# Placing the larger half of the ranked experts nine places apart instead of one

## The chip, the cores and the metric

The kernel runs on one core of one Trainium2 chip. The metric is the device time of one execution in microseconds (us); lower is shorter. A measurement is the median of several executions.

## What is computed

The reference is one layer of a diffusion backbone: a token mixer (retention and mLSTM over 512 latent tokens) followed by a mixture of experts. Only the second half matters here:

```
p_g = softmax(u @ w_rg + b_rg); g_idx = top_k(p_g, 1)
le  = (u @ w_re + b_re) of that group's 8 experts
pe_top, e_idx = top_k(softmax(le), 2)          # 2 experts of 32 for each of 512 tokens
expert(x) = (silu(x @ w_e1[e]) * (x @ w_e3[e])) @ w_e2[e]
out = sum over a token's two experts of weight * expert(token)
```

So 1,024 assignments are spread over 32 experts, unevenly, and the order in which experts are worked off is free. Each expert has three weight matrices of 2 MB in float32.

## The kernel before

The token mixer fills the first 1,000 us or so. Then comes a routing part (who goes to which expert), then a loop over 32 *places* `e`, each of which works one expert off, then the combination of the results and the last norm.

**A place.** An expert's tokens are cut into blocks of 32. The number of blocks, `n`, is read at run time into a register; every place has code for one block, and branches over the code for a second, a third and further blocks. A block is: `hidden_q` (line 1483: one pass of 64 matrix instructions over `w_e1` and `w_e3`), an activation, a small transpose (line 1473), and `output_q` (line 1494: 32 matrix instructions over `w_e2`). The first two blocks' tokens are fetched three places ahead by an indirect gather (`fetch_both`, tile `xr`); tokens of a third and further block are fetched inside the place (`rows`, tile `xo`). Results are stored to `y_d` by GpSimd's queue (lines 1651 and 1654, and 1514 for a third and further block). At the end of a conditional part each engine waits and branches; lines 1519, 1523, 1643 and 1652 are such ends and line 1629 is the load of the next place's `n`.

**The weights.** `load(n)` (line 949) issues load `n` of 96 on SyncE's queue (SP), in the order of the places, three loads a place, into a ring of 11 buffers. Load `3e + 11` and the two after it are issued when place `e` has released its buffers, so loads run up to about three and a half places ahead; and a load waits for the landing of the load three before it, so at most three are under way. For places from 4 on the expert's number is read from the tile `place[0]`.

**The order of the places.** Places 0 to 3 are experts 0 to 3 (`SET` is 4). The other 28 experts are ranked by their number of tokens, largest first, in ranks 4 to 31 (tile `ov`). The larger half, ranks 4 to 17, takes the even places 4, 6, ..., 30 in rank order; the smaller half, ranks 18 to 31, takes the odd places from 31 down to 5. So a large and a small expert alternate and the largest come first. The ranks become places in a dozen VectorE instructions on tiles of 128x32 (lines 1566 to 1572); from the places follow `yrow` and `pos` (where an assignment's result and its token number are kept), a scatter of the token numbers (line 1595, GpSimd), their reading back (line 1617), the gathers, and `place`.

Of the kernel before, what the change touches and what calls it, by code (L numbers as in the profile page):

```python
# [12 lines left out]
I32 = mybir.dt.int32  # L13
AF = mybir.ActivationFunctionType
OP = mybir.AluOpType
# [4 lines left out]
P = 128  # L20
# [5 lines left out]
NE = 32  # L26
# [3 lines left out]
SET = 4  # L30
# [38 lines left out]
def build(tc, I, out, dbg=None):  # L69
    nc = tc.nc  # L70
    V, S, G, PE, SP = nc.vector, nc.scalar, nc.gpsimd, nc.tensor, nc.sync
# [856 lines left out]
    loads, place, turn_of = [], [], {}  # L928
# [67 lines left out]
    eoff = moec.tile([P, NE], F32, name="eoff")  # L996
# [423 lines left out]
    m1p = mo.enter_context(tc.tile_pool(name="m1p", bufs=1, reuse_waits="tile"))  # L1420
# [10 lines left out]
    def slots_in(n, b):  # L1431

        xT = slots_of(b)
        for a in range(4):
            V.tensor_copy(xT[:, :, a, :], xg[a][:, :, n, 32 * b:32 * b + 32])
        return xT
# [99 lines left out]
    with tc.manual_schedule(engines={EN.DVE}):  # L1536
        xnext = [slots_in(0, b) for b in range(2)]
        ov = m1p.tile([P, NE], F32, tag="ov", name="ov")
        V.tensor_scalar(ov, nblk, -2.0, 0.0, op0=OP.add, op1=OP.max)
        V.scalar_tensor_tensor(ov, ov, 0.5, ov, op0=OP.is_gt, op1=OP.add)  # L1540
        nil = m1p.tile([P, NE], F32, tag="nil", name="nil")
        V.memset(nil, 0.0)
        V.tensor_tensor_scan(obase, ov, nil, 0.0, op0=OP.add, op1=OP.add)
        V.tensor_sub(obase, obase, ov)
        V.tensor_scalar(ocol, obase, 2.0 * NE, None, op0=OP.add)
        V.tensor_scalar(obase, obase, 32.0, 64.0 * NE, op0=OP.mult, op1=OP.add)

        key = m1p.tile([P, NE], F32, name="key")
        V.scalar_tensor_tensor(key, cnt, 2048.0, eoff, op0=OP.mult, op1=OP.subtract)
        V.tensor_scalar(key[:, 0:SET], eoff[:, 0:SET], -1.0, 1.0e7, op0=OP.mult, op1=OP.add)  # L1550
        val = m1p.tile([P, NE], F32, name="val")
        V.tensor_scalar(val, ocol, 1024.0, None, op0=OP.mult)
        V.scalar_tensor_tensor(val, nblk, 32.0, val, op0=OP.mult, op1=OP.add)
        V.scalar_tensor_tensor(val, eoff, 1.0 / 64, val, op0=OP.mult, op1=OP.add)

        def beside(a, b, n):

            return (a.rearrange("p (i o) -> p i o", o=1).to_broadcast([P, n, NE]),
                    b.rearrange("p (o j) -> p o j", o=1).to_broadcast([P, n, NE]))

        for a in range(2):
            h = slice(16 * a, 16 * a + 16)
            M = mr.tile([P, 16, NE], F32, tag="yt", name="M", bufs=YB)
            V.tensor_tensor(M, *beside(key[:, h], key, 16), op=OP.is_lt)
            V.reduce_sum(ov[:, h], M, axis=AX.X)
        V.tensor_scalar(nil, ov, SET - 0.5, None, op0=OP.is_gt)
        V.scalar_tensor_tensor(nil, ov, float(-SET), nil, op0=OP.add, op1=OP.mult)
        V.tensor_scalar(key, ov, (NE + SET) / 2 - 0.5, None, op0=OP.is_gt)
        V.tensor_scalar(eoff, ov, -4.0, 2.0 * (NE + SET) - 1, op0=OP.mult, op1=OP.add)
        V.tensor_mul(key, key, eoff)  # L1570
        V.tensor_add(ov, ov, nil)
        V.tensor_add(ov, ov, key)
        V.tensor_scalar(eoff, ov, 64.0, None, op0=OP.mult)
        sel = m1p.tile([P, 3, 8], F32, name="sel")
        rr = mr.tile([P, 8, NE], F32, tag="yq", name="rr", bufs=1)
        E8 = Ea.rearrange("p i k e -> p (i k) e")
        for a, src in enumerate((eoff, obase)):
            V.tensor_mul(rr, E8, src.rearrange("p (o e) -> p o e", o=1).to_broadcast([P, 8, NE]))
            V.reduce_sum(sel[:, a, :], rr, axis=AX.X)
        r8 = rank.rearrange("p i k -> p (i k)")  # L1580
        V.scalar_tensor_tensor(sel[:, 1, :], sel[:, 1, :], -64.0, sel[:, 0, :], op0=OP.add, op1=OP.subtract)
        V.tensor_scalar(sel[:, 2, :], r8, 63.5, None, op0=OP.is_gt)
        V.tensor_mul(sel[:, 1, :], sel[:, 1, :], sel[:, 2, :])
        V.tensor_add(sel[:, 0, :], sel[:, 0, :], sel[:, 1, :])
        V.tensor_add(yrow.rearrange("p i k -> p (i k)"), sel[:, 0, :], r8)
        rb8 = m1p.tile([P, 8], I32, name="rb8")
        V.tensor_copy(rb8, r8)
        V.tensor_scalar(rb8, rb8, 5, None, op0=OP.logical_shift_right)
        V.tensor_scalar(sel[:, 0, :], sel[:, 0, :], 1.0 / 32, None, op0=OP.mult)
        V.scalar_tensor_tensor(sel[:, 0, :], r8, float(NC), sel[:, 0, :], op0=OP.mult, op1=OP.add)  # L1590
        pos = m1p.tile([P, 8], I32, name="pos")
        V.scalar_tensor_tensor(pos, rb8, 1.0 - 32 * NC, sel[:, 0, :], op0=OP.mult, op1=OP.add)
# [7 lines left out]
    with tc.manual_schedule(engines={EN.DVE}):  # L1600
        V.tensor_scalar(ov, ov, 1.0, None, op0=OP.add)
        for a in range(2):
            h = slice(16 * a, 16 * a + 16)
            M = mr.tile([P, 16, NE], F32, tag="yt", name="M", bufs=YB)
            at, by = beside(iota[:, h], ov, 16)
            V.tensor_tensor(M, at, by, op=OP.is_equal)
            V.tensor_mul(M, M, beside(iota[:, h], val, 16)[1])
            V.reduce_sum(key[:, h], M, axis=AX.X)
        place += [m1p.tile([P, NE], I32, name=f"place{a}") for a in range(3)]
        V.tensor_copy(place[0], key)  # L1610
        V.tensor_scalar(place[1], place[0], 5, None, op0=OP.logical_shift_right)
        V.tensor_scalar(place[2], place[0], 10, None, op0=OP.logical_shift_right)
        V.tensor_scalar(place[0], place[0], 31, None, op0=OP.bitwise_and)
        V.tensor_scalar(place[1], place[1], 31, None, op0=OP.bitwise_and)
# [140 lines left out]
```

## Time and profile before

| | |
|---|---|
| three executions | 1661.69, 1650.82, 1650.40 us |
| median | 1650.82 us |
| the profiled execution | 1648.84 us |
| its span, first to last instruction | 1647.2 us |
| TensorE busy (matmul) | 1336.8 us, 81% of the span |
| VectorE / ScalarE / GpSimd busy | 773.8 / 425.8 / 296.3 us |
| moved by DMA | 355.31 MB, of it 96 weight loads of 2,048 KB |

The profile comes from one execution. Its page gives busy times, the span in 40 equal slices (41.2 us each), the DMA queues, and groups of instructions by line. Other views of the trace list single instructions in order of time, who waited for whom, and the busy time in chosen stretches. Times in those views count from the first instruction. PE is TensorE, DVE VectorE, ACT ScalarE, POOL GpSimd; a name with a q behind it (PEq) is that engine's instruction sequencer, and an idle time put down to it was ended by a branch, a semaphore or a register instruction, not by a tile.

### The profile page before, as it was taken

How to read it: one execution, taken by the hardware profiler on the slowest of the kernel's cores; microseconds unless marked ns; L12 is line 12 of the kernel's file. 1: busy time of each engine (PE TensorE's matmuls, PEld its weight loads, DVE VectorE, ACT ScalarE, POOL GpSimd, SP SyncE). 2: the span in 40 equal slices, each digit the busy share in tenths (PEclk: the TensorE clock that was granted, in tenths of full speed). 3: DMA queues.
4: the chain of work that ended last, by engine and by line, in shares of the span. 5: the costliest groups of instructions: out<-in, count | busy, mean ns of one | idle time of the engine just before them, and what ended most of it. 6: DMA issues, size and time to landing. Idle time of an engine off the chain costs nothing. (4 is left out here: it accounts for less than half of the span.)

```text
span 1647.2 us, 27521 instructions
## 1 busy us (share of the span) xinstructions
PE 1336.8 (81%) x10733; PEld 1029.2 (62%) x10733; DVE 773.8 (47%) x1857; ACT 425.8 (26%) x764; POOL 296.3 (18%) x249
## 2 busy tenths in 40 slices
PE   5999899999999999999998965556757666666574
PEld 3797888989798998989886753223323333333331
DVE  6657366485656566564778796111111111111115
ACT  3432244253444444444433120000000000000001
POOL 0100055143100000000012243222221211212103
PEclk9999999999999999999999977778888789988887
DMA  9414985243412122121655685955669999999974
GB/s 350 132 60 121 298 251 167 75 158 119 111 60 71 58 90 65 58 71 52 211 173 184 230 348 209 394 207 196 238 269 402 372 404 374 403 375 410 408 297 156
DMA packets 160928, 355.31 MB, mean 216 GB/s; under 512 B 24476, under 2 KB 111724, under 8 KB 152472
## 3 DMA queue, kind: packets, MB, share of 16 engines
q1 hardware_dynamic: 147736, 328.40, 54.6%
q0 software_dynamic: 11632, 19.54, 3.5%
q10 hardware_dynamic: 1296, 4.19, 0.6%
q8 instruction: 125, 2.05, 0.5%
q14 instruction: 139, 1.14, 0.2%
HBM read 316.34 MB, written 35.69 MB: 214 GB/s over the span
## 5 line engine op out<-in xcount | busy, mean ns | idle before, releaser
L1483 PE MATMUL ps_h<-w,xT 128*32 128x256 f32 x3072 | 222.8, 446 | 102.9 <-PEq L1629 49.9
L1483 PEld LDWEIGHTS ps_h<-w,xT 128*32 128x32 f32 x3072 | 123.0, 128 | 205.8 <-issue 127.3
L194 DVE TENSOR_TENSOR w_lo<-raw,w_hi 128x1024 fp32r<-128x1024 f32 x96 | 129.1, 1368 | 30.3 <-ACT w_hi L193 30.3
L1464 ACT ACTIVATE t<-ps_h 64x256 f32<-64x256 f32 x48 | 18.1, 377 | 480.3 <-PE ps_h L1483 429.2
L1452 DVE COPY xT<-ps_x 128x256 f32<-128x256 f32 x63 | 26.3, 417 | 231.9 <-PE ps_x L1450 222.5
L1494 PE MATMUL ps_y<-w,hT 128*32 128x256 f32 x1536 | 117.9, 459 | 20.4 <-ACT hT L1475 17.5
L193 ACT ACTIVATE w_hi<-raw 128x1024 fp32r<-128x1024 f32 x96 | 96.1, 1050 | 62.1 <-PE ps_t L214 18.0
L907 POOL TENSOR_TENSOR raw<-raw,g 128x2048 f32<-128x2048 f32 x4 | 18.6, 4642 | 451.9 <-DMA brw<-br_d 417.7
L557 POOL TENSOR_TENSOR macc<-macc,mw 128x1024 f32<-128x1024 f32 x32 | 79.6, 2487 | 96.8 <-ACT mw L556 88.7
L1496 DVE TENSOR_TENSOR yt<-ps_y,g2q 128x256 f32<-128x256 f32 x43 | 18.2, 424 | 165.9 <-PE ps_y L1494 131.5
L1494 PEld LDWEIGHTS ps_y<-w,hT 128*32 128x32 f32 x1536 | 52.0, 126 | 63.2 <-ACT hT L1475 23.3
L1442 POOL DMA_INDIRECT xr<-u_d,inv x56 | 58.0, 1036 | 181.8 <-DMA y_d<-yt 57.1
L213 PE MATMUL ps_q<-u_lat,w_hi 128*128 128x512 f32 x192 | 79.5, 414 | 2.4 <-ACT u_lat L319 1.7
L214 PE MATMUL ps_q<-u_lat,w_hi 128*128 128x512 f32 x192 | 78.8, 410 | 0.0
L215 PE MATMUL ps_q<-u_lat,w_lo 128*128 128x512 f32 x192 | 78.4, 409 | 0.0
L1473 PE MATMUL ps_ht<-small,t 64*128 64x64 f32 x96 | 15.2, 239 | 76.9 <-DVE t L1466 72.7
L213 PE MATMUL ps_v<-w_hi,u_lat 128*128 128x256 f32 x256 | 72.1, 282 | 0.0
L214 PE MATMUL ps_v<-w_lo,u_lat 128*128 128x256 f32 x256 | 72.1, 282 | 0.0
L215 PE MATMUL ps_g<-w_hi,u_lat 128*128 128x256 f32 x256 | 72.1, 282 | 0.0
L215 PE MATMUL ps_v<-w_hi,u_lat 128*128 128x256 f32 x256 | 72.1, 281 | 0.0
L213 PE MATMUL ps_g<-w_hi,u_lat 128*128 128x256 f32 x256 | 72.1, 281 | 0.0
L214 PE MATMUL ps_g<-w_lo,u_lat 128*128 128x256 f32 x256 | 72.0, 281 | 0.0
(429 smaller groups left out, 3433.9 us busy)
## 6 DMA issues: line engine op xcount, KB each, us to landing
w<-in_w_e_dram SPq DMA_DIRECT2D x96, 2048.0 KB
raw<-in_w_in_dram SPq DMA_DIRECT2D x40, 1024.0 KB
mw<-in_w_ada_dram SPq DMA_DIRECT2D x32, 512.0 KB
y_d<-plain SPq DMA_DIRECT2D x28, 512.0 KB
wada<-in_w_ada_dram SPq DMA_DIRECT2D x4, 2048.0 KB
y_d<-yt POOLq DMA_DIRECT2D x43, 128.0 KB
tanh_d<-tg SPq DMA_DIRECT2D x16, 256.0 KB
br_d<-rt SPq DMA_DIRECT2D x16, 256.0 KB
```

The costliest lines, as they stand in the source:

```text
L193: S.activation(h_, r_, AF.Copy)
L194: V.tensor_sub(l_, r_, f32(h_))
L213: PE.matmul(ps, lh, rh, start=first, stop=False)
L214: PE.matmul(ps, lh, rl, start=False, stop=False)
L215: PE.matmul(ps, ll, rh, start=False, stop=last)
L557: G.tensor_add(acc, acc, w)
L907: G.tensor_mul(raw, raw, g1.rearrange("p (o f) -> p o f", o=1).to_broadcast([P, NK, 256]))
L1442: G.indirect_dma_start(out=xr, out_offset=None, in_=u_d, in_offset=bass.IndirectOffsetOnAxis(ap=at, axis=0), bounds_check=4 * T - 1, oob_i ...
L1452: V.tensor_copy(xT.rearrange("p c a s -> p c (a s)"), pt)
L1483: PE.matmul(ps[32 * a:32 * a + 32, 0:256], x[:, kt % 2, kt // 2, :], w[a // 2][:, kt, 256 * (a % 2):256 * (a % 2) + 256], start=(kt == 0), ...
L1494: PE.matmul(py[32 * a:32 * a + 32, 0:256], hT[:, kt % 2, 32 * (kt // 2):32 * (kt // 2) + 32], w2[:, kt, 256 * a:256 * a + 256], start=(kt ...
L1496: V.tensor_mul(yq, py[:, 0:256], g2q)
```

## The change

The odd places and places 0 to 3 stay as they are. Among the larger half, rank `4 + j` goes to place `4 + 2 * (9 j mod 14)` in place of `4 + 2 j`. The even places 4, 6, ..., 30 thus hold ranks 4, 15, 12, 9, 6, 17, 14, 11, 8, 5, 16, 13, 10, 7, where before they held ranks 4, 5, 6, ..., 17. The quotient of `9 j` by 14 is computed with a multiplication and a shift in an integer tile; for that the three `place` tiles are made earlier, and the first of them is used as scratch.

```
@@ after the ranks are counted into ov
+        place += [m1p.tile([P, NE], I32, name=f"place{a}") for a in range(3)]
+        ninths = place[0]
+        V.tensor_scalar(ninths, ov, 9.0 * 4682, -9.0 * 4682 * SET, op0=OP.mult, op1=OP.add)
+        V.tensor_scalar(ninths, ninths, 16, None, op0=OP.logical_shift_right)
         V.tensor_scalar(nil, ov, SET - 0.5, None, op0=OP.is_gt)
-        V.scalar_tensor_tensor(nil, ov, float(-SET), nil, op0=OP.add, op1=OP.mult)
+        V.tensor_scalar(eoff, ov, 17.0, SET - 18.0 * SET, op0=OP.mult, op1=OP.add)
+        V.scalar_tensor_tensor(eoff, ninths, -28.0, eoff, op0=OP.mult, op1=OP.add)
+        V.tensor_mul(nil, nil, eoff)
         V.tensor_scalar(key, ov, (NE + SET) / 2 - 0.5, None, op0=OP.is_gt)
-        V.tensor_scalar(eoff, ov, -4.0, 2.0 * (NE + SET) - 1, op0=OP.mult, op1=OP.add)
+        V.scalar_tensor_tensor(eoff, ov, 3.0, eoff, op0=OP.mult, op1=OP.add)
+        V.tensor_scalar(eoff, eoff, -1.0, 2.0 * NE + 3, op0=OP.mult, op1=OP.add)
         V.tensor_mul(key, key, eoff)
         V.tensor_add(ov, ov, nil)
         V.tensor_add(ov, ov, key)
@@ further down, where place is filled
-        place += [m1p.tile([P, NE], I32, name=f"place{a}") for a in range(3)]
         V.tensor_copy(place[0], key)
```

## Rows read from the trace of the kernel before

**Rows 1.** The page's 40 slices: busy share of the DMA engines, in tenths

```profile
DMA  9414985243412122121655685955669999999974
```

**Rows 2.** Busy times by stretch: stretch, length, engines, granted clock, DMA share, GB/s

```profile
1091.70:1129.50 37.80, 22.68 (x338) 11.63 (x334) 6.23 (x15) 2.62 (x8) 11.88 (x20) 0.91 0.12 33
...
1170.00:1184.60 14.60, 11.12 (x102) 4.83 (x102) 1.79 (x5) 0.65 (x2) 2.42 (x4) 0.63 0.06 20
1184.60:1221.30 36.70, 18.67 (x302) 11.09 (x302) 5.47 (x14) 1.96 (x6) 10.84 (x15) 0.91 0.96 381
1221.30:1234.30 13.00, 9.29 (x102) 4.29 (x102) 1.76 (x5) 0.65 (x2) 2.42 (x4) 0.72 0.09 27
...
1265.00:1586.00 321.00, 206.69 (x2669) 111.61 (x2673) 47.05 (x124) 17.01 (x52) 54.87 (x60) 0.86 0.98 394
```

**Rows 3.** Waits of SP, 1133 to 1606 us: total us, times, longest

```profile
SPq L949 <- PEq L1519: 50.9, 2, 27.1
```

**Rows 4.** Line 949's instructions, whole run: who waited for the loads

```profile
  PE ps_h L1483: 10.4, 1
```

**Rows 5.** Waits of PE, 1133 to 1606 us: total us, times, longest

```profile
PE ps_h L1483 <- PEq L1629: 49.9, 14, 5.6
...
PE ps_x L1450 <- DMA xo<-u_d,ix: 12.8, 2, 10.6
```

**Rows 6.** PE by line, stretches 1133.5-1245.6, 1245.6-1513, 1513-1605: count, busy, idle before

```profile
L1483 PE MATMUL ps_h<-w,xT 128*32 128x256 f32 x576 | 41.7, 452 | 13.1 <-issue 5.5 <-PEq L1629 3.6 <-DVEq L1519 2.9
...
L1483 PE MATMUL ps_h<-w,xT 128*32 128x256 f32 x1472 | 104.7, 434 | 44.5 <-PEq L1629 32.0 <-issue 6.8 <-DVEq L1643 5.6
...
L1483 PE MATMUL ps_h<-w,xT 128*32 128x256 f32 x448 | 35.0, 466 | 21.9 <-PEq L1629 14.2 <-DVEq L1643 4.4 <-issue 3.3
```

**Rows 7.** PE in order of time, first passes of places: start, us, idle before

```profile
1133.95 6.55 PE L1483 MATMUL ps_h<-w,xT 128*32 128x256 f32 x64 [5.46 <-issue]
1150.50 5.12 PE L1483 MATMUL ps_h<-w,xT 128*32 128x256 f32 x64 [3.62 <-PEq L1629]
...
1185.88 3.66 PE L1483 MATMUL ps_h<-w,xT 128*32 128x256 f32 x64 [1.46 <-DVEq L1519]
1195.40 3.66 PE L1483 MATMUL ps_h<-w,xT 128*32 128x256 f32 x64 [1.11 <-DVEq L1643]
...
1246.70 1.89 PE L1483 MATMUL ps_h<-w,xT 128*32 128x256 f32 x27 [1.15 <-DVEq L1643]
...
1265.79 5.50 PE L1483 MATMUL ps_h<-w,xT 128*32 128x256 f32 x64 [1.34 <-PEq L1629]
1280.73 6.55 PE L1483 MATMUL ps_h<-w,xT 128*32 128x256 f32 x64 [4.69 <-PEq L1629]
...
1446.54 5.35 PE L1483 MATMUL ps_h<-w,xT 128*32 128x256 f32 x64 [3.67 <-PEq L1629]
...
1457.76 1.89 PE L1483 MATMUL ps_h<-w,xT 128*32 128x256 f32 x27 [1.12 <-DVEq L1643]
...
1514.19 5.88 PE L1483 MATMUL ps_h<-w,xT 128*32 128x256 f32 x64 [5.28 <-PEq L1629]
...
1550.35 3.66 PE L1483 MATMUL ps_h<-w,xT 128*32 128x256 f32 x64 [1.09 <-DVEq L1643]
...
1594.92 3.66 PE L1483 MATMUL ps_h<-w,xT 128*32 128x256 f32 x64 [1.07 <-DVEq L1643]
```

**Rows 8.** In order of time: the gathered third blocks of places 6 and 8

```profile
1170.91 0.66 PE L1450 MATMUL ps_x<-small,xo 128*128 128x128 f32 x2 [2.24 <-DMA xo<-u_d,ix]
...
1222.48 0.66 PE L1450 MATMUL ps_x<-small,xo 128*128 128x128 f32 x2 [10.59 <-DMA xo<-u_d,ix]
```

**Rows 9.** In order of time: ranks become places, then the scatter

```profile
1011.49 0.17 DVE L1566 TENSOR_SCALAR nil<-ov 128x32 f32<-128x32 f32 x1
...
1012.65 0.18 DVE L1573 TENSOR_SCALAR eoff<-ov 128x32 f32<-128x32 f32 x1
...
1019.69 1.19 POOL L1595 DMA_INDIRECT inv_d<-owni,pos  x1 [22.39 <-DVE pos L1592]
```

## The prediction

> **What bounds the kernel now.** I read the slices of the page first, because the change moves experts inside one stage only. After slice 29 of 40 the DMA engines stand at 9 tenths or more up to the last but two slices, and before that they dip to 5 and 6 [rows 1]. This looks like a stage that is bound by loading weights and that wastes DMA time in its first third. The table by stretch says where: from 1091.7 to 1129.5 us the DMA share is 0.12, from 1170.0 to 1184.6 it is 0.06, from 1221.3 to 1234.3 it is 0.09, and from 1265 to 1586 it is 0.98 [rows 2]. SP's waits name the cause of the second and the third: 50.9 us in two waits for the end of a conditional part of the kind that only places with three blocks or more run (line 1519) [rows 3]. A large expert keeps its ring buffers, and the loads behind it stand still.
>
> The question is who waits for the weights. Over the whole run the answer is one wait of 10.4 us [rows 4], which is at place 4, ahead of everything that moves. Among PE's waits from 1133 to 1606 us there is none for a weight; what is there is 49.9 us in 14 waits that PE's own sequencer ends at the start of a place, and 12.8 us in two waits for a gather [rows 5]. So the idle DMA time was taken out of a lead, not out of the time. PE goes from place to place without a stop for loads up to the end, and the stage lasts as long as PE's places, added up.
>
> How many blocks the places run follows from the pass counts (64 instructions a pass). Places 5 to 9 make 576/64 = 9 passes, places 10 to 24 make 1472/64 = 23, places 25 to 31 make 448/64 = 7 [rows 6]. In order of time they are: place 4 five blocks, 6 and 8 three each, 10, 12, ..., 24 two each (eight), 26 to 30 one, every odd place one. As rank order before was place order, rank 4 has five blocks, ranks 5 and 6 three, 7 to 14 two, 15 to 17 one.
>
> **The change part by part.** The places' new contents follow from the list of ranks: place 4 five blocks as before; 6, 14 and 24 one; 8, 10, 16, 18, 20, 26, 28 and 30 two; 12 and 22 three. Everything up to the end of place 5 stays. The same 39 blocks stand in places 5 to 31, in another order, so I add up PE's time by kinds of neighbours, from first pass to first pass [rows 7].
>
> Before: place 5 takes 1150.50 - 1133.95 = 16.55 us. A three-block place with the single after it takes 1195.40 - 1150.50 = 44.90 (places 6, 7) and 1246.70 - 1195.40 = 51.30 (8, 9). Place 10 takes 1265.79 - 1246.70 = 19.09. Places 11 to 24, seven pairs of a single and a two-block place, take 1514.19 - 1265.79 = 248.40, or 35.49 a pair. The six singles 25 to 30 take 80.73: the first three 1550.35 - 1514.19 = 36.16, or 12.05 each, the last three 44.57, or 14.86 each. The sum to the first pass of place 31 is 460.97 us.
>
> After:
> - place 5: 16.55.
> - singles behind a single or ahead of one (6, 7, 14, 15, 24, 25): six. They come in runs of two, with place 5 of three, so I take the first three of the old run: 6 x 12.05 = 72.3. The other end is the last three, 89.2.
> - pairs (8 and 9, 10 and 11, 16 to 21, 26 to 29): seven, 248.4.
> - three-block places with their single (12 and 13, 22 and 23): between 2 x 44.90 and 2 x 51.30. The difference between the two old ones is mostly the wait for the gathered third block, 2.24 us in place 6 and 10.59 in place 8 [rows 8]. GpSimd issues that gather behind its work for the place before; ahead of place 6 stood a single of 16.55 us, ahead of place 8 one of 1195.40 - 1185.88 = 9.52. The singles ahead of the new ones took 1280.73 - 1265.79 = 14.94 (place 11) and 1457.76 - 1446.54 = 11.22 (place 21) [rows 7], one near each. So I take the old sum, 96.2, with 6.4 up or down.
> - place 30, two blocks alone: a pair less a single, 35.49 - 12.05 = 23.44; the other end is place 10's 19.09.
>
> The sum is 456.9, which is 4.1 less than before; at the bounds 446.1 to 480.2.
>
> Are the weights still early enough? The loads of a place's first pass are issued when the place four before it ends, so three places lie between. At their shortest these are singles of 12.05, 36 us; three loads are 3 x 2.10 MB, at 394 GB/s [rows 2] 16 us. That leaves a margin of 20. A single gives the loads only 12.05 of their 16 us, so a run of three (5, 6, 7) puts them some 8 us behind; a pair gives 35.5 for 32 and takes it back. So loads keep ahead, by less in places 6 to 11 than now, and DMA is idle in place 12 and in place 22 in place of 6 and 8.
>
> The VectorE part: seven instructions become twelve. The old seven start at 1011.49 and what follows them at 1012.65 [rows 9], 0.17 us each; five more are 0.8 us. They lie on the path: the scatter at 1019.69 had waited for the positions that follow from them, 22.39 us [rows 9], and the gathers of places 4 and 5 follow the scatter. The bounds are nothing (if place 4 starts by its wait of 10.4 us for something else [rows 4]) and 1.1 (five at the 0.22 us that chained ones may take, an estimate from the same row's spread). I take 0.8. The three `place` tiles are made earlier but written by the same engine in order; if their memory was still being read, the wait would end by 1018, when the old code wrote them, at most 6 us; as the tiles around them are written at that time without a wait, I take nothing. The integer tile holds 9 j times 4682 at most 547,794, exactly, and 4682/65536 gives the quotient by 14 right for j up to 13, so the order is the one the text of the change says. No queue is passed and no DMA is added.
>
> Sum: -4.1 + 0.8 = -3.3. The profiled execution took 1648.84 us, 2.0 under the median; taken from the median of 1650.82 it gives 1647.5 us.
>
> **The rivals.** I call a difference of more than 1%, 16.5 us, one that can be told from no change: under 1634.3 or over 1667.3.
>
> First, *the weights are the bound after all* (faster). Then the idle stretches of places 6 and 8, 14.6 + 13.0 = 27.6 us [rows 2], come off the end: 1623. For it speaks the share of 0.98 up to 1586 [rows 2]; against it that no place after 4 waits for a load [rows 4, 5]. Chance 0.10.
>
> Second, *fewer or more waits at branches*. The 14 sequencer waits take 3.6 us each [rows 5], and the pass behind one runs slower: 6.55 us after a wait of 5.46, 3.66 after one of 1.11 [rows 7]. So one such start costs 6.5 us. Nine places get another number of blocks and so leave through another branch. Three waits fewer give 1647.5 - 19.4 = 1628, three more give 1667. Nothing in the rows says that one order has fewer; the three dear singles at the end (14.86) may be of this kind, and the sum has them gone already. Chance 0.09 for three or more fewer, 0.05 for three or more additional ones.
> The Trainium skill, page "Runtime: NRT & Kernel Launch", section "Instruction fetch mechanics", says that instructions come in blocks over DMA, fetched ahead in order, and that a taken branch out of the blocks at hand has to wait for a fetch. The waits above look like that. By this rule the single places, which jump over the most code, should each pay, in any order.
>
> Third, *the gather of a third block lands late* (slower). In places 12 and 22 the load queue has been full for long. Place 8 ran beside loads as well, at a share of 0.96 [rows 2], and waited 10.59. If the two waited twice that, 21.2 each in place of 12.8 together, the time is 1647.5 + 29.6 = 1677. From 16.3 us each it decides for slower. Chance 0.10.
>
> The page "DMA: Bandwidth & Descriptors" of the Trainium skill, section "Where 436 GB/s comes from", puts the limit of one core's reading of HBM at about 358 GB/s; the stretch of 321 us here moved 394 [rows 2], so the measurement decides. At 358 three loads would be an estimated 17.6 us, and the margin above 18.
>
> **How the numbers follow.** No change that can be told: 0.66, with a range of its own of 1637 to 1666 (some of the bounds above together). Faster: 0.10 + 0.09 = 0.19. Slower: 0.10 + 0.05 = 0.15. The range for 8 in 10 has to hold the first rival's 1623 and the three-waits cases (1628, 1667) and leaves out the late gather: 1622 to 1668.
>
> **What would show it.** Right: still no wait of PE for a weight after place 4; the low DMA shares moved to places 12 and 22, together about as long; the stretch from place 5 to place 31 within a few us of 457; the third blocks' gathers waiting 2 to 11 us. Wrong: waits of PE for line 949 in places 8 to 11 (loads the bound); sequencer waits of PE far from 14 or from 50 us; gather waits over 16 us; a start of place 5 later than 1135.

## The result, and the profile after

The changed kernel is slower: 1665.22 us median of 10 runs against 1650.61 of 10 runs of the kernel before, ratio 1.0094 with a 95% interval of 1.0067 to 1.0120. Its profiled execution took 1662.07 us, with a span of 1660.4; before it was 1648.84 and 1647.2. So the two profiles differ by 13.2 us, the medians by 14.6. The prediction was 1647.5, a gain of 3.3 us; the run shows a loss.

Where the 13.2 us lie is read from the first passes of the places, TensorE in order of time (start, us, what it did, idle time before and what ended it). From line 1610 on the changed kernel's line numbers are 7 higher (line 1636 is 1629 of [rows 7], 1650 is 1643), between 1573 and 1608 they are 8 higher.

```profile
1136.53 6.56 PE L1483 MATMUL ps_h<-w,xT 128*32 128x256 f32 x64 [5.40 <-issue]
1153.12 5.11 PE L1483 MATMUL ps_h<-w,xT 128*32 128x256 f32 x64 [3.63 <-PEq L1636]
1164.10 3.65 PE L1483 MATMUL ps_h<-w,xT 128*32 128x256 f32 x60 [1.11 <-DVEq L1650]
...
1178.35 6.14 PE L1483 MATMUL ps_h<-w,xT 128*32 128x256 f32 x64 [4.77 <-PEq L1636]
...
1249.35 6.47 PE L1483 MATMUL ps_h<-w,xT 128*32 128x256 f32 x64 [4.90 <-PEq L1636]
...
1296.46 1.89 PE L1483 MATMUL ps_h<-w,xT 128*32 128x256 f32 x27 [1.12 <-DVEq L1650]
...
1309.48 5.43 PE L1483 MATMUL ps_h<-w,xT 128*32 128x256 f32 x64 [1.09 <-DVEq L1650]
1324.63 6.38 PE L1483 MATMUL ps_h<-w,xT 128*32 128x256 f32 x64 [4.96 <-PEq L1636]
...
1436.64 3.25 PE L1483 MATMUL ps_h<-w,xT 128*32 128x256 f32 x27 [5.04 <-PEq L1636]
...
1488.59 6.32 PE L1483 MATMUL ps_h<-w,xT 128*32 128x256 f32 x64 [4.68 <-PEq L1636]
1505.83 6.24 PE L1483 MATMUL ps_h<-w,xT 128*32 128x256 f32 x64 [4.64 <-PEq L1636]
1521.83 3.33 PE L1483 MATMUL ps_h<-w,xT 128*32 128x256 f32 x27 [5.01 <-PEq L1636]
...
1587.11 1.89 PE L1483 MATMUL ps_h<-w,xT 128*32 128x256 f32 x27 [1.16 <-DVEq L1650]
...
1608.08 3.66 PE L1483 MATMUL ps_h<-w,xT 128*32 128x256 f32 x64 [0.95 <-DVEq L1659]
```

These are the starts of places 5, 6, 7, 8, 12, 14, 15, 16, 22, 24, 25, 26, 30 and 31; x27 and x60 mark passes of 64 that break and go on a little later. Place 5 starts at 1136.53, 2.6 us later than before; from there to place 31 it is 471.55 us where it was 460.97, +10.6; behind that start both spans have 52.3 us left. So 10.6 of the 13.2 us lie in the stretch in which the order of the experts changed, in these two executions.

TensorE's waits between 1136 and 1619 us (line it waited on, releaser: total us, times, longest) answer [rows 5]:

```profile
PE ps_h L1483 <- PEq L1636: 60.3, 15, 5.1
...
PE ps_h L1483 <- issue: 17.1, 9, 5.4
...
PE ps_h L1483 <- DVEq L1650: 8.3, 7, 1.6
PE ps_x L1450 <- DMA xo<-u_d,ix: 6.6, 2, 3.3
PE ps_h L1483 <- PEq L1650: 4.9, 1, 4.9
```

The waits that TensorE's own sequencer ends grew from 49.9 us in 14 to 60.3 + 4.9 = 65.2 in 16. The two gathers got cheaper, 6.6 us for 12.8. Nothing here is a weight: over the whole run there is again a single wait for a load, at place 4 (14.0 us where [rows 4] has 10.4), and SP stands still twice, as in [rows 3]. From line 949's own instructions, and from SP's waits:

```profile
  PE ps_h L1483: 14.0, 1
```

```profile
SPq L949 <- PEq L1519: 45.0, 2, 23.3
```

The DMA engines' busy share in 40 slices of the stretch from place 5 to place 31 (11.8 us each) shows the idle stretches at places 12 and 22 and nearly full slices elsewhere:

```profile
DMA  9899999999942999999997999993299999999960
```

So the loads did what was predicted, and the time went another way: more of it is lost where one place ends and the next begins. I call the idle time of TensorE in front of a place's first pass its *gap*, and say that the exit of the place before waits when the gap is over 2.2 us; an exit that doesn't wait shows 0.7 to 2.2 us. Added up over places 6 to 31 the gaps are 78.5 us (before: 63.9), and of the 26 exits of places 5 to 30 14 wait (before: 10). A long gap is followed by a slow pass. Two first passes, of places 8 and 13, by stretch (stretch, length, busy times, granted TensorE clock, DMA share, GB/s):

```profile
1178.40:1184.40 6.00, 6.00 (x64) 3.01 (x64) 0.00 (x0) 0.00 (x0) 0.13 (x1) 0.58 1.00 408
1286.90:1290.50 3.60, 3.58 (x64) 2.38 (x64) 0.00 (x0) 0.00 (x0) 1.51 (x3) 1.00 0.85 309
```

Behind a gap of 4.77 us the granted clock is 0.58 on average, most of the pass at the lower of its two levels (1.2 GHz), and the same 64 instructions take 6.1 us in place of 3.7.

### The profile page after: what moved, and what is told of

Same layout as the page of the kernel before. It is cut to its first block, busy times and chain, and to the rows that moved or that the text cites. A ratio compares the mean times of both kernels' runs of the same rounds, so it can differ in the third digit from the quotient of the medians.

```text
span 1660.4 us, 27526 instructions
## 1 busy us (share of the span) xinstructions
PE 1345.3 (81%) x10733; PEld 1033.1 (62%) x10733; DVE 772.7 (47%) x1862; ACT 426.1 (26%) x764; POOL 295.7 (18%) x249
## 3 DMA queue, kind: packets, MB, share of 16 engines
q8 instruction: 125, 2.05, 0.5%
## 5 line engine op out<-in xcount | busy, mean ns | idle before, releaser
L1483 PE MATMUL ps_h<-w,xT 128*32 128x256 f32 x3072 | 227.8, 453 | 122.2 <-PEq L1636 60.3
L193 ACT ACTIVATE w_hi<-raw 128x1024 fp32r<-128x1024 f32 x96 | 96.2, 1051 | 63.2 <-PE ps_t L214 18.0
L907 POOL TENSOR_TENSOR raw<-raw,g 128x2048 f32<-128x2048 f32 x4 | 18.7, 4666 | 452.3 <-PE ps_b L215 418.6
L557 POOL TENSOR_TENSOR macc<-macc,mw 128x1024 f32<-128x1024 f32 x32 | 79.1, 2471 | 95.8 <-ACT mw L556 87.9
## 6 DMA issues: line engine op xcount, KB each, us to landing
wada<-in_w_ada_dram SPq DMA_DIRECT2D x4, 2048.0 KB, 11.9
```

What stands on the lines that cost most here:

```text
L193: S.activation(h_, r_, AF.Copy)
L557: G.tensor_add(acc, acc, w)
L907: G.tensor_mul(raw, raw, g1.rearrange("p (o f) -> p o f", o=1).to_broadcast([P, NK, 256]))
L1483: PE.matmul(ps[32 * a:32 * a + 32, 0:256], x[:, kt % 2, kt // 2, :], w[a // 2][:, kt, 256 * (a % 2):256 * (a % 2) + 256], start=(kt == 0), ...
```

## The experiments

All of them start from the changed kernel. "One place on" is that kernel with the old order (counted in even places, as "nine places on" is); its instructions are the new ones, so it keeps the five added VectorE steps.

**The order alone.**

```diff
-V.tensor_scalar(ninths, ov, 9.0 * 4682, -9.0 * 4682 * SET, ...)
+V.tensor_scalar(ninths, ov, 1.0 * 4682, -1.0 * 4682 * SET, ...)
...
-V.tensor_scalar(eoff, ov, 17.0, SET - 18.0 * SET, ...)
+V.tensor_scalar(eoff, ov, 1.0, SET - 2.0 * SET, ...)
```

> The changed kernel with its three constants set for a step of one place: the same instructions, the order of before. Theory A (the loss is in PE's waits at branches, which come with the order of the places): ratio to before 1.000 to 1.002, PE's sequencer and issue waits at first passes near 65 us as before. Theory B (the loss is in the five added VectorE instructions, which hold up the scatter and the first gathers): ratio near 1.009, as the change itself, with place 5 starting 4 us late or more. Between them, 1.003 to 1.006, both have a part.

Measured: 1656.18 us, ratio to the kernel before 1.0031 (1.0003 to 1.0059). By the medians about two thirds of the loss go with the order. To see whether it is this order or any other, the constants for thirteen places on (rank 5 at place 30, rank 6 at 28, and so down):

> Step of 13 places, which is the larger half in reverse behind the largest: five blocks, then three singles, eight places of two blocks, and the two of three blocks at places 28 and 30. Theory A: the number of waits at branches decides; a count of waits at first passes of 65 us gives 1650, of 82 us gives 1665. Rival E (the loads fall behind in a run of singles, from 5 to 11 here): PE waits for line 949 in places 9 to 13, and the time is over 1675.

Measured: 1662.23 us, ratio 1.0070 (1.0041 to 1.0098), with gaps of 76.3 us. It is not special to nine.

**The VectorE steps alone.** One place on, with 20 steps more of the kind that the change adds, on the same path:

```diff
+for _ in range(20):
+    V.tensor_scalar(ov, ov, 0.0, None, op0=OP.add)
```

> One place on, with 20 more VectorE steps of one column in the chain that makes the offsets. If such a step costs what its record shows and no more (0.17 to 0.22 us): +3.4 to +4.4 us against one place on, 1660 (ratio 1.005 to 1.006). If the five steps that the change adds explain the whole 0.3% between one place on and the kernel before (about 1 us each): +20 us, 1676 (ratio 1.015). If they are hidden: 1656.

Measured: 1653.83 us, ratio 1.0019 (0.9988 to 1.0051). Twenty steps cost nothing that can be seen, so five don't cost 5 us; the 1.0031 above holds scatter between builds and runs of one order. With a third kernel of that order, whose branch hints come later (below, 0.9975), the mean of the three is 1.0008.

**The exits: what they wait for.** Ahead of a pass a place tells TensorE which way the branch behind it will go (the three `tc.mark_branch_hint_location` lines). Without these hints, in both orders:

```diff
-tc.mark_branch_hint_location(f"more{e}d", smin(n >> 2, 1), engines={EN.PE})
...
-tc.mark_branch_hint_location(f"more{e}a", smin(n >> 1, 1), engines={EN.PE})
...
-tc.mark_branch_hint_location(f"more{e}c", smin(n // 3, 1), engines={EN.PE})
```

> Step of one place, and all three branch hints taken out. Theory A: a place's exit that did not wait in the old order had its code brought by the hint; without hints nearly all 27 exits of places 5 to 31 wait, some 17 more than in the old order at about 6.5 us each: 60 to 110 us slower, 1.04 to 1.07. Rival C (the waits are not about fetched code, but about the other engines' ends of the conditional parts): no hint matters, ratio within 1.005.

> Step of nine places, without branch hints. Theory A: with every exit waiting in both orders, the two orders come out alike, within 5 us of the step of one without hints. Rival D (the order costs by something that has to do with blocks, gathers or loads and not with branches): it stays 13 to 16 us over the step of one without hints.

Measured: one place on 1711.67 us, 1.0357 (1.0299 to 1.0414); nine places on 1717.31, 1.0402 (1.0349 to 1.0456). The two orders are 5.6 us apart, where theory A had put under 5 and rival D 13 to 16, and their intervals overlap, so this pair doesn't decide between them. TensorE's largest wait, one place on and then nine:

```profile
PE ps_h L1483 <- PEq L1635: 122.6, 23, 9.9
```

```profile
PE ps_h L1483 <- PEq L1635: 128.9, 23, 10.4
```

Now all 26 exits of places 5 to 30 wait, 5.3 and 5.6 us on average in these groups, in either order. So what is waited for comes with the branch, and with the hints in place some exits still wait as if they had none.

What is it that takes 5 us? Instructions are brought by DMA queues of their own; one of them carries 16.4 KB a packet, in the list of queues from place 5 to place 31 of the changed kernel (queue, kind: packets, MB, share of 16 engines):

```profile
q8 instruction: 64, 1.05, 0.9%
```

That is 1.05 MB / 64 = 16.4 KB a packet, on DMA engines whose busy share is 0.90, most of it loads. The trace's records of these packets say that the exits do wait for them: behind all 14 exits that wait, the first pass starts 2.5 to 3.0 us after such a packet has landed, and in 13 of the 14 it lands inside the gap. To take the loads' traffic away, each load brings only half of its matrix and the passes use that half twice; half of the products are left out, TensorE's instructions stay the same:

```diff
-loads.append(SP.dma_start(t, src))
+h = 4 if m < 2 else 2
+loads.append(SP.dma_start(t[:, 0:h], src[:, 0:h]))
...
-w[a // 2][:, kt, 256 * (a % 2):256 * (a % 2) + 256],
+w[a // 2][:, kt % 4, 256 * (a % 2):256 * (a % 2) + 256],
...
-w2[:, kt, 256 * a:256 * a + 256], start=(kt == 0), stop=(kt == 3))
+w2[:, kt % 2, 256 * a:256 * a + 256], start=(kt == 0), stop=(kt == 3))
```

> Step of nine; every weight load brings half of its matrix (the first half of its rows), and the passes use that half twice, so the instructions on PE are the same and half of the products are left out. Theory A (exits wait because a fetch of code over a busy DMA takes some 5 us and the one in flight makes the hint come to nothing): with DMA half empty the waits of PE's sequencer and issue at first passes fall from 82 us to under 45, and the time to 1615 to 1640. Rival F (what the branches cost has nothing to do with the loads): the waits stay near 80 us and the time within 6 us of the change's 1665.

> Step of one place with the same halved loads and products. Theory A: the waits fall as well, and the two orders stand within 4 us of each other. Rival D (the order costs by its blocks, not by what the loads do to fetches): 8 to 12 us under the step of nine, as with whole loads.

Measured: nine places on 1560.95 us, 0.9447 (0.9387 to 0.9506); one place on 1559.24, 0.9393 (0.9341 to 0.9444). That is far below the 1615 to 1640 put on record. The sequencer's waits, nine places on:

```profile
PE ps_h L1484 <- PEq L1637: 20.2, 10, 3.9
```

This group falls from 60.3 us in 15 to 20.2 in 10, and the gaps from 78.5 us to 41.2 (one place on: 47.1). No pass behind place 4 had waited for a weight, and yet from place 5 to place 31 it is 393.0 us in place of 471.5; of these 78.5 us 37.3 are gaps. TensorE's busy time is 26.2 us less (276.9 for 303.1, at a granted clock of 0.90 for 0.84), and its other waits 15.0 us, of which 6.6 are the gathers. The stage is TensorE's in the sense that TensorE never waits for a weight; it is still the loads that make it long, for the gaps because TensorE's instructions come over the same engines. Whether the higher clock follows from the shorter gaps alone was not tried. The packets themselves take no longer beside whole loads: 1.1 us at the median in both kernels. What differs is when they start: with whole loads 12 of the 14 packets behind a wait start after TensorE has gone idle, with half loads, both orders together, 11 of 14 start no later than that. Between the two orders the medians are 1.7 us apart here; the intervals of the two ratios overlap.

**Is a hint lost because it comes too early?** Both hints moved behind the fourth of the eight steps of the pass:

```diff
-tc.mark_branch_hint_location(f"more{e}a", smin(n >> 1, 1), engines={EN.PE})
-t0 = hidden_q(xT[0], w, gated("t0"))
+t0 = hidden_q(xT[0], w, gated("t0"),
+              lambda: tc.mark_branch_hint_location(f"more{e}a", smin(n >> 1, 1), engines={EN.PE}))
```

> Step of nine, whole loads; each branch hint stands behind half of the pass of the block ahead of the branch (64 instructions' first 32) in place of ahead of it. Theory A: a hint that is given while a fetch is in flight comes to nothing; half a pass later that fetch is mostly over, so most exits that waited 5 us wait 1 to 3 us; waits at first passes fall from 82 to 50 or less, time 1630 to 1650. Rival G (the hints come too late for a place of one block as it is): later hints make more exits wait, and the time goes up towards the 1717 of no hints.

> Step of one place with the same later hints. Theory A: as with the step of nine, 1630 to 1650, the two within 5 us of each other. Rival G: over 1670.

Measured: nine places on 1666.43 us, 1.0057 (1.0032 to 1.0082), gaps 77.3 us, 15 exits wait; one place on 1651.67, 0.9975 (0.9941 to 1.0009), gaps 67.9, 12 exits. The same exits wait, but for a few, and no time is gained where 1630 to 1650 had been put on record; half a pass in the moment of the hint is not the reason. That idea fell.

**Which exits wait.** Set in a table by place number, all kernels so far that have hints and whole loads show one pattern. From place 8 on, exits of places whose number leaves 0 on division by 4 wait (2.8 to 5.7 us) if the place has one or two blocks, and not if it has three (at most 1.5). Those that leave 2 show 2.6 us at most, and most of them 1.0 to 1.7. The odd ones go by what precedes them: behind a one-block place that leaves 2, for instance, 8 of 10 wait. An order of block counts alone can't make a period of four places; where the code of a place lies can. To shift all code from place 4 on, without any work, transposes go into a loop body at place 3 that is never entered, 64 of them (128 TensorE instructions with their weight loads), 32 or 96:

```diff
-def facing(xr, b, pool, tag):
+def facing(xr, b, pool, tag, times=1):
...
-    for c in range(2):
+    for c in [0, 1] * times:
...
-some(base + i - 2, facing(rows(base + i - 2), 2, tps, "tp"))
+some(base + i - 2, facing(rows(base + i - 2), 2, tps, "tp", 33 if e == 3 else 1))
```

> The order of before (one place on) with the instructions of the changed kernel and the same 128 idle instructions ahead of place 4. Theory of the code's position: 10, 14, 18, 22 wait at their end, and 12, 16, 20, 24 no more; 6 with its three blocks does not wait, and 8 with three does not either; 26 and 30 wait; time within 1% of one place on without the idle instructions (1656). Rival (order of block counts alone): the same places as without the idle instructions, gaps 68 us.

> The changed kernel (nine places on), with 128 TensorE instructions more in a loop body that is never entered, ahead of place 4: it shifts the code of all later places by 128 instructions and adds no work. Theory (whether the exit of a place waits hangs on where its code lies, with a period of four places): the places whose number leaves 0 and 2 on division by 4 change roles. The one- and two-block places 6, 10, 14, 18, 26 and 30 then wait 3.4 to 5.7 us at their end, and 8, 16, 20, 24 and 28 about 1.2. The sum of the gaps stays between 70 and 90 us and the time within 1% of the changed kernel's. Rival (the wait hangs on the order of block counts alone): the same places wait as in the changed kernel (8, 16, 20, 24, 28 at 4 to 5 us), with the same sum of gaps, 78 us.

> One place on with 64 idle instructions, half of that shift. Theory of the code's position: the places at which the exit waits move to others again, to a pattern that is neither that without idle instructions nor that with 128; time between 1635 and 1670, a size that this theory cannot give. Rival: no difference to one place on (1656, gaps 68 us, the same places wait).

First passes behind places 16, 18 and 20, one place on without idle instructions and then with 128 of them:

```profile
1372.81 6.10 PE L1483 MATMUL ps_h<-w,xT 128*32 128x256 f32 x64 [5.02 <-PEq L1636]
...
1411.81 5.39 PE L1483 MATMUL ps_h<-w,xT 128*32 128x256 f32 x64 [1.41 <-PEq L1636]
...
1444.83 5.94 PE L1483 MATMUL ps_h<-w,xT 128*32 128x256 f32 x64 [5.70 <-PEq L1636]
```

```profile
1385.88 3.66 PE L1483 MATMUL ps_h<-w,xT 128*32 128x256 f32 x64 [1.33 <-PEq L1636]
...
1422.16 5.67 PE L1483 MATMUL ps_h<-w,xT 128*32 128x256 f32 x64 [4.69 <-PEq L1636]
...
1456.31 5.66 PE L1483 MATMUL ps_h<-w,xT 128*32 128x256 f32 x64 [1.40 <-PEq L1636]
```

The same places, the same two blocks each, the same neighbours: where 16 and 20 waited, 18 waits. With nine places on it is likewise (6, 10, 14, 18 and 26 wait, 16, 20, 24 and 28 don't). Not as put on record are the three-block places 6 and 8 one place on, which waited 3.2 and 2.7 us, place 8 nine places on, with 4.1, and place 30, which waited in neither. With 64 idle instructions the exits behind 16, 17, 18 and 19 are:

```profile
1378.70 5.31 PE L1483 MATMUL ps_h<-w,xT 128*32 128x256 f32 x64 [6.62 <-PEq L1636]
1394.36 6.01 PE L1483 MATMUL ps_h<-w,xT 128*32 128x256 f32 x64 [5.59 <-PEq L1636]
1414.11 3.66 PE L1483 MATMUL ps_h<-w,xT 128*32 128x256 f32 x64 [1.38 <-PEq L1636]
1423.63 3.65 PE L1483 MATMUL ps_h<-w,xT 128*32 128x256 f32 x60 [1.10 <-DVEq L1650]
```

A third pattern: two neighbours wait, two don't. With 192 it is this one shifted by two places. So that an exit waits hangs on where the code lies; that is shown. It doesn't hang on that alone: the exit of 27 waited one place on (4.8 us) and not with the 20 VectorE steps more (1.1), with the same TensorE code. The Trainium skill, page "Runtime: NRT & Kernel Launch", section "Instruction fetch mechanics", has instructions come in blocks of 16 KiB, 256 of them; the packets of 16.4 KB agree, and 128 instructions would be half a block, as the swap of roles has it.

Measured times: one place on with 128 1654.72 us, 1.0015 (0.9988 to 1.0043); nine places on with 128 1661.44, 1.0047 (1.0015 to 1.0080); one place on with 64 1654.75, 1.0013 (0.9987 to 1.0038). By the medians the order still costs, though with 128 its gaps are no longer (73.6 us against 75.7); but the two intervals with 128 overlap.

**Is the price of the order in the exits?** If so, it should vanish where the pattern hardly hangs on block counts, with 64 and 192 idle instructions.

> Nine places on, with 64 idle instructions ahead of place 4. One place on with the same 64 waited at the end of nearly all places whose number leaves 0 or 1 on division by 4 and at none that leaves 2 or 3 (gaps 86 us, ratio 1.001). Theory A (the order costs time only through the exits that wait): here the pattern hangs so little on block counts that both orders wait alike: 9, 13, 16, 17, 20, 21, 25, 28 and 29 wait, 6, 7, 10, 11, 14, 15 don't, gaps 80 to 90 us, and the ratio to the kernel before is that of one place on, 1.001 (0.998 to 1.004). Theory B (the order costs 0.5% by something else, the granted clock of the passes or when the weights stream): the same exits wait, and the ratio is still 1.006 (1.003 to 1.010).

> Nine places on, with 192 idle instructions: half a period on from 64. Theory of the code's position: the exits of places that leave 2 or 3 on division by 4 wait (7, 10, 11, 14, 15, 18, 19, 23, 26, 27), those that leave 0 or 1 don't. Theory A (above): the same ratio as one place on with 192 idle instructions, within 0.3%. Theory B: 0.5% more than that.

> One place on, with 192 idle instructions. Theory of the code's position: 7, 10, 11, 14, 15, 18, 19, 22, 23, 26 and 27 wait, gaps near 86 us, ratio 1.001 as with 64. Rival: the pattern of no idle instructions, gaps 64 to 69 us.

> The kernel with nine places on and 128 idle instructions once more, beside the three above: its profiled run had an order effect (478.1 us from place 5 to place 31 against 470.5 with one place on) though the gaps were no longer (73.6 and 75.7 us). If that was one execution's scatter: ratio near 1.002 and 468 to 472 us. If the order has a price apart from the gaps: ratio 1.005 and 475 to 480 us again, with longer first passes (145 us) and places (259 us).

| idle instructions | one place on | nine places on | gaps, us, one / nine |
|---|---|---|---|
| 0 | 1.0031 | 1.0094 | 68.7 / 78.5 |
| 0, late hints | 0.9975 | 1.0057 | 67.9 / 77.3 |
| 64 | 1.0013 | 1.0074 | 86.2 / 89.9 |
| 128 | 1.0015 | 1.0047 and 1.0028 | 75.7 / 73.6 and 74.2 |
| 192 | 0.9956 | 1.0048 | 84.8 / 84.6 |

(Medians of the four: 1670.69, 1663.19, 1649.50, 1660.48 us; intervals 1.0050 to 1.0098, 1.0021 to 1.0074, 0.9930 to 0.9983, 1.0001 to 1.0055.) All exits that were put on record wait. Against the pattern some others do too: nine places on those of 6, 14 and 26 (with 64) and 24 (with 192), one place on those of 13 and 28 (with 192, 2.6 and 3.0 us). In each row of the table nine places on is the slower, by 0.1 to 0.9%. With 128 that is within the intervals; with 192 it is clear of them, with equal gaps (84.8 and 84.6 us). Theory A, that the order costs only through waiting exits, falls. The stretch from place 5 to place 31 (length, TensorE busy, granted clock, DMA share, GB/s) with 64 idle instructions, one place on and then nine:

```profile
1139.20:1596.80 457.60, 282.64 (x3836) 0.87 0.93 371
```

```profile
1135.60:1618.10 482.50, 299.35 (x3836) 0.83 0.89 352
```

TensorE idles 482.5 - 299.35 = 183.2 us in place of 175.0, and is busy 16.7 us longer at a lower clock. With 192 the idle times are 183.2 and 174.4. With 128 they are 169.4 and, in the repeat, 175.6 against 164.8; without any, 168.5 against 164.8, and with late hints 172.0 against 157.7. So idle time goes up by 4 to 14 us in each pair, at some positions in the gaps, at others in the waits for the gathered third blocks (17.4 us in place of 11.1 with 192). The repeat says how far one profile can be trusted: 478.1 us and then 471.2 for the same kernel, with TensorE busy for 308.7 and 295.5, so that what the first showed apart from the gaps was scatter for the greater part.

One place on with 192 idle instructions is the one kernel here that beats both: 1649.50 us, 0.9956, an interval below 1. It has the old order, with its code in another place, and is no gain of the change.

**Which half of the new order costs.** Nine places on sends the three-block experts from places 6 and 8 to 12 and 22, and the one-block ones from 26, 28 and 30 to 6, 14 and 24. Something like each alone, by swapping single ranks of one place on:

```diff
+swap = m1p.tile([P, NE], F32, name="swap")
+for r, by in ((11, -12.0), (5, 12.0), (12, -6.0), (9, 6.0)):
+    V.tensor_scalar(swap, ov, SET + r, by, op0=OP.is_equal, op1=OP.mult)
+    V.tensor_add(eoff, eoff, swap)
 V.tensor_mul(nil, nil, eoff)
```

That seats one-block experts at 14, 22 and 30; with the pairs (1, 16), (9, -16), (2, 4), (4, -4) the three-block ones sit at 12 and 22.

> Half of the change in order: one place on, but two of the three one-block experts from places 26 and 28 change seats with the two-block ones at 14 and 22. The three-block experts stay at 6 and 8. Theory 1 (the one-block experts among the others cost the time: behind each of them at a place that leaves 2 on division by 4 the next exit waits too): 15 and 23 wait in addition, gaps 72 to 80 us, ratio to the kernel before 1.006 (1.003 to 1.009). Theory 2 (what costs is that the three-block experts come late): gaps 64 to 69 us, ratio 1.001 (0.998 to 1.004).

> The other half: one place on, but the two three-block experts change seats with the two-block ones at 12 and 22, where the changed kernel has them; the one-block experts stay last (26, 28, 30). Theory 1: gaps 64 to 70 us, ratio 1.001 (0.998 to 1.004). Theory 2: ratio 1.006 (1.003 to 1.009), with place 5 to place 31 at 470 us or more. If both halves give 1.003, the two add up.

Measured: one-block experts spread 1656.20 us, 1.0020 (0.9998 to 1.0042); three-block experts late 1658.28, 1.0036 (1.0014 to 1.0057). The first did to the exits what was put on record (15 waits in addition, 23 as it had one place on; gaps 74.9 us) and cost next to nothing in time. Gaps of the second are 72.5 us, its stretch from place 5 to place 31 is 472.0. The times of both lie in the ranges of theory 2, that the late three-block experts cost; the gaps are those of neither theory. Against the mean of 1.0008 for one place on the first excess, 0.1%, lies within its interval, the second, 0.3%, just outside (1.0014 is its lower end). The traces point the same way: over all executions with hints and whole loads but that of thirteen places on, the two three-block places with the single behind each take 98.3 to 108.9 us where they stand at 12 and 22 (mean 102.3), and where they stand at 6 and 8 94.1 to 96.7, but for one with 104.1 (mean 96.6). So a part of the price lies there, not the whole: the two excesses add up to about half of the 0.8% and more that the changed kernel has.

## Why the prediction was wrong, point by point

The 1647.5 was an answer of the wrong sign. That the loss of 14.6 us is still under the 16.5 us that the prediction called no change, and 1665.22 inside its range of 1622 to 1668, is luck as far as the sum goes.

**The sum over kinds of places: the step that failed.** Its terms beside what the profiles have, in us from first pass to first pass (one-block places in runs; the three-block places with the single behind each; seven pairs; the two-block place that stands alone):

| | place 5 | six singles | three-block | pairs | alone | sum |
|---|---|---|---|---|---|---|
| predicted | 16.6 | 72.3 | 96.2 | 248.4 | 23.4 | 456.9 |
| changed kernel | 16.6 | 86.6 | 99.1 | 248.3 | 21.0 | 471.5 |
| the same, late hints | 15.0 | 83.9 | 102.6 | 253.8 | 18.7 | 474.0 |
| kernel before | 16.6 | 80.7 | 96.2 | 248.4 | 19.1 | 461.0 |
| one place on | 16.7 | 87.9 | 96.4 | 243.6 | 23.0 | 467.6 |
| one place on, late hints | 15.0 | 85.4 | 94.1 | 245.2 | 21.5 | 461.2 |
| one place on, 20 more steps | 14.8 | 80.1 | 95.2 | 251.8 | 18.7 | 460.6 |

The sum misses by 14.6 us, and one term is off by 14.3, the singles; the three-block places (+2.9) and place 30 (-2.4) cancel, and that the pairs hit to 0.1 us is luck, as they scatter from 243.6 to 253.8 below. The prediction had two ends for it, 72.3 and 89.2, and took the first three of the old run, 12.05 us each, because they stood next to a two-block place. What made those three cheap is not their neighbour: none of their exits waited in that one execution (gaps of 1.2, 1.1 and 1.1 us in the trace of before). One place on, the same three places behind the same neighbours took 13.7, 11.8 and 15.1 us, with the 20 steps more 11.9, 12.2 and 11.8. In the changed kernel the exits of 7, 15, 24 and 25 wait. A price per kind of place was the wrong unit. It needed the place number beside the block count, and the trace of before already had it: the exits of 12, 16, 20, 24 and 28 waited (20 for 3.67, 24 for 5.28 us [rows 7]), those of 10, 14, 18, 22 and 26 did not, though 12 to 24 all have two blocks.

The table also says how much of the 10.6 us is scatter. Over the four executions of the old order the mean is 462.6, over the two of the new 472.8. The three-block places are dearer in both of the new (99.1 and 102.6 against 94.1 to 96.4), the other terms overlap. Of the 10.2 us between the means 5.4 are the three-block places, 3.8 the pairs and 1.7 the singles. So the singles explain why the sum missed; they are nearly as dear in the old order, and are not what makes the new one slower.

**Rival two, another number of waits at branches.** That was the mechanism of the sum's miss, with the sign that had 0.05: sequencer waits from 14 to 16, two more and not three, and the total from 49.9 to 65.2 us, since they are longer too. Its price of 6.5 us each was of the right size: 60.3 / 15 = 4.0 us of wait and, behind a long one, 6.1 - 3.6 = 2.5 us of slow pass. What the prediction lacked was what decides which exits wait; it said that nothing in the rows speaks for more or fewer. The rule of the Trainium skill named there would have had each single place pay in any order. By these runs all pay without the hints (26 of 26 exits wait), and with them it hangs on the position.

**The loads.** No wait for a weight behind place 4, idle DMA stretches at 12 and 22, SP held twice for 45.0 us: all as predicted. But "the stage lasts as long as TensorE's places" hides what half the loads showed: the loads set how many exits wait and for how long. The first rival, that the idle DMA time comes off the end, did not come.

**The gathers.** 6.4 us up or down was allowed on the old 12.8; it was -6.2, in order of time 3.29 and 3.27:

```profile
1274.98 0.41 PE L1450 MATMUL ps_x<-small,xo 128*128 128x128 f32 x2 [3.29 <-DMA xo<-u_d,ix]
...
1461.80 0.66 PE L1450 MATMUL ps_x<-small,xo 128*128 128x128 f32 x2 [3.27 <-DMA xo<-u_d,ix]
```

The third rival did not come. One place on had 13.0, 4.3 and 13.0 us in three executions, nine places on 6.6 to 17.4, so this term scatters by more than what was argued from the single ahead.

**The VectorE steps.** The twelve steps (seven before), from the first to what follows them, in order of time:

```profile
1010.43 0.17 DVE L1569 TENSOR_SCALAR place<-ov 128x32 int32<-128x32 f32 x1
...
1012.48 0.18 DVE L1581 TENSOR_SCALAR eoff<-ov 128x32 f32<-128x32 f32 x1
```

2.05 us where it was 1.16, +0.9 for a predicted 0.8, and no wait for the tiles made earlier. The scatter of the changed kernel:

```profile
1019.52 1.20 POOL L1603 DMA_INDIRECT inv_d<-owni,pos  x1 [23.74 <-DVE pos L1600]
```

From the first step to the scatter it is 9.09 us where [rows 9] has 8.20, and 13.85 with the 20 steps more. So the steps do lie on the path to the scatter, as predicted; that it starts no later than before (1019.69) is only because this execution came to the first step 1.1 us earlier. Behind the scatter nothing shows them: 20 steps more left the time where it was. So no run shows the 0.8 us in the time.

Place 5 did start later than 1135, at 1136.53, which the prediction had named as a sign against it; the kernels with the old order and the new instructions start it between 1136.0 and 1142.1. What the traces show is the first pass of place 4, before and then after:

```profile
1078.05 5.50 PE L1483 MATMUL ps_h<-w,xT 128*32 128x256 f32 x64 [10.38 <-DMA w<-in_w_e_dram]
```

```profile
1082.03 6.50 PE L1483 MATMUL ps_h<-w,xT 128*32 128x256 f32 x64 [14.04 <-DMA w<-in_w_e_dram]
```

Its weights came later, though SP began to issue loads in this part of the run 1.0 us earlier (1017.97 for 1018.95). Whether that is scatter of the two executions or the new instructions wasn't tried.

**What stays open.** Shown are: that the exits wait for instructions, that the loads set how many wait and for how long, and that the position of the code decides, for most, which. That nine places on is slower than one place on is seen in every pair, at four positions; with 128 idle instructions, without hints and with half loads the intervals overlap. Why it is, beyond the gaps of the unshifted code (+10 us in both pairs there), is not settled: idle time grows at each position, but in different waits, and neither half of the order has the whole. The late three-block places are dearer nearly throughout (102.3 us for 96.6), but what makes them so was not tried; the waits for their gathers, 6.6 to 17.4 us for 4.3 to 13.0, overlap.

## What to carry to other kernels

Before costing a reordering by kinds of work, look whether the price of one kind has a period in the place number; if it has, the code's position is part of the price, and the sum must go by place and kind. A stage in which no pass waits for a load can still be made long by loads, if the instructions of its branches come over the same DMA engines, and a kernel with half the traffic shows it. A difference of 10 us that rests on one profile of each side is little more than what two profiles of one kernel differ by (478.1 and 471.2 here).

## What the hardware showed that was not expected

- Instructions that never run move the waits of others: shifting the code by 128 of them moved the exits that wait by two places, although each exit had its hint. One place on, the gaps were 66 to 69 us without a shift, 76 with 128, 85 with 192 and 86 with 64, and the times still lay within 0.8% of each other.
- Where the code lies shows in a pass too: in the changed kernel the first passes of places 10, 14, 18, 22, 26 and 30 break after instruction 27 of 64, for 0.6 to 2.0 us. One place on with 128 idle ones those of 12, 16, 20, 24 and 28 do so, for 0.8 to 2.3 us; 16 and 20 are:

```profile
1364.84 1.89 PE L1483 MATMUL ps_h<-w,xT 128*32 128x256 f32 x27 [1.09 <-DVEq L1650]
...
1433.74 1.89 PE L1483 MATMUL ps_h<-w,xT 128*32 128x256 f32 x27 [1.15 <-DVEq L1650]
```

- In the group of waits that the sequencer ends, one without hints took 5.3 us on average (one place on, DMA share 0.84), one with hints 4.0 us (nine places on, 0.90), and one with hints and half the loads 2.0 us (20.2 in 10, share 0.64).
- A first pass that waited started 2.5 to 3.0 us after the landing of an instruction packet of 16.4 KB that itself took 1.1 us at the median, with half the loads as with whole ones (both kernels with nine places on and hints).
